# Feed forward's first product: eleven pairs of offsets of the weight parts, a transpose ahead of each unit's products

## The chip, the cores and the metric

The kernel runs on one core of one Trainium2 chip. The metric is the device time of one execution in microseconds (us): 1716.87 us is the median of two runs of the kernel before, 1713.42 and 1720.32 us. All products run on TensorE (PE in the profile). PE first loads 128 x 128 stationary weights (its own row in the profile, PEld) and then streams the moving operand through them, at most 512 columns a time, into a PSUM tile.

## The reference

Two transformer blocks for 256 tokens of width 2048, in float32. The first has attention with a forget gate, a short convolution, pooling and layer norm. The second has gated linear attention, then the feed forward that this change touches, then a gate and a final norm. Cut to that part:

```python
def swiglu(hn, w_in, w_out):
    gate, up = jnp.split(jnp.einsum('btd,de->bte', hn, w_in), 2, axis=-1)
    return jnp.einsum('btf,fd->btd', jax.nn.silu(gate) * up, w_out)

h = h + swiglu(rmsnorm(h, ffn_norm[i]), ffn_w_in[i], ffn_w_out[i])
```

`w_in` is 2048 x 11264: 44 tiles of 128 features for the gate and 44 for the up half.

## The kernel before, in words

Every large product is split so that the fast format fp32r keeps nearly float32 accuracy. A weight tile arrives by DMA as `raw` (128 x 2048, 1 MB), ScalarE (ACT) rounds it to fp32r into `whi` (line 77), and VectorE (DVE) subtracts to get the rest, `wlo` (line 85). The activations lie in SBUF the same way, as a high and a low half side by side (`x[:, k]`, 512 columns: 256 tokens high, 256 tokens low). In the feature-major form, `fm_mm`, which the change touches, a **unit** is one weight tile of 16 slices of 128 x 128. Each slice makes one **pair** of products: the high weights times all 512 columns (line 185), then the low weights times the 256 high columns (line 187). In the token-major form, `tm_mm` (lines 208 to 210), the activations are the stationary operand and the weights move.

A class `Stream` sets the order of everything. Units are listed in program order; the DMA for a unit is issued three units ahead, its high and low part are made two units ahead, and the work that follows a unit's products (its `post`) comes ahead of the next unit's products. Pools of three buffers each hold `raw`, `whi` and `wlo`. Each buffer of `whi` and `wlo` has 64 columns more than the 2048 that are used (`PAD`). In every feature-major unit `whi` starts 16 columns into its buffer (`SHIFT`, line 24; the slice is in line 76) and `wlo` starts at column 0; token-major units have both at 0. A column is 4 bytes on each partition.

The feed forward's first product is 88 units, for f = 0 to 43 a gate and an up, in two parts (48 units for f < 24, then 40), each followed by units of the second product. The function `ffn_in` lists them (lines 1093 and 1094). `gate` and `up` are their posts: ACT and DVE add the two halves of the PSUM tile, scale, apply the activation and split the result into `g`. For f = 0 the token scale is not known yet when the gate is ready; `spread` (line 269) lays it over all partitions with two small fp32 products between the second and the third unit. Ahead of that, inside the first unit, eight transposes (line 1008) of the last quarter of the activations are mixed into the products. The PSUM tiles of these small products come from a pool of four (`axps`), those of the units from another four (`mmps`).

Of the kernel before, what the change touches and what calls it, by code (L numbers as in the profile page):

```python
# [9 lines left out]
F32R = mybir.dt.float32r  # L10
# [7 lines left out]
P = 128  # L18
S = 256
D = 2048  # L20
KT = D // P
UN = 2048

PAD, SHIFT = 64, 16
ALPHA = 2.0 ** 0.25
BIG = 3.0e38

# [7 lines left out]
ORDER = "HFPTL"  # L35
# [4 lines left out]
class Stream:  # L40
# [30 lines left out]
    def _hi(self, w):  # L71
        if w < len(self.ws):
            n, pre_split = self.ws[w][1], self.ws[w][5]
            if pre_split is not None:
                pre_split()
            hi = self.hi_p.tile([P, UN + PAD], F32R, tag="whi", name="whi")[:, self.ws[w][8]:]
            self.nc.scalar.copy(hi[:, :n], self.raw[w][:, :n])  # L77
            self.parts[w] = [hi]

    def _lo(self, w):  # L80
        if w < len(self.ws):
            n, eng = self.ws[w][1], self.ws[w][6]
            t, hi = self.raw.pop(w), self.parts[w][0]
            lo = self.lo_p.tile([P, UN + PAD], F32R, tag="wlo", name="wlo")
            eng.tensor_tensor(lo[:, :n], t[:, :n], hi[:, :n], op=ALU.subtract)  # L85
            self.parts[w].append(lo)
        self._load(w + self.raw_bufs)
# [48 lines left out]
def program(ctx, tc, a, out):  # L136
    nc = tc.nc
# [14 lines left out]
    st = Stream(nc, raw_p, hi_p, lo_p, 3, 2)  # L152

    def mmps():
        return ps_mm.tile([P, 512], F32, tag="mm", name="mm")

    def axps():
        return ps_ax.tile([P, 512], F32, tag="ax", name="ax")

    ident = const.tile([P, P], F32, name="ident")  # L160
# [16 lines left out]
    def fm_mm(ps, hi, lo, x, k0, n, first, last, m=P, zigzag=False):  # L177


        for kk in range(n):  # L180
            w, k = slice(kk * m, (kk + 1) * m), k0 + kk
            if kk and zigzag:
                MM(ps[:, :S], lhsT=lo[:, w], rhs=x[:, k, 0], start=False, stop=False)
            end = last and kk == n - 1
            MM(ps, lhsT=hi[:, w], rhs=x[:, k], start=first and kk == 0, stop=end and zigzag)  # L185
            if not kk or not zigzag:
                MM(ps[:, :S], lhsT=lo[:, w], rhs=x[:, k, 0], start=False, stop=end and not zigzag)  # L187
            for fn in mid.pop(kk, ()):
                fn()

    def join(dst, ps):

        A.copy(dst, ps[:, S:])
        V.tensor_tensor(dst, ps[:, :S], dst, op=ALU.add)  # L194

    def split(x, k, src):

        A.copy(x[:, k, 0], src)
        V.tensor_tensor(x[:, k, 1], src, x[:, k, 0], op=ALU.subtract)
# [9 lines left out]
                MM(ps2[t], lhsT=x[:, k0 + kk, 0, tok], rhs=lo[:, w], start=False, stop=False)  # L209
                MM(ps2[t], lhsT=x[:, k0 + kk, 1, tok], rhs=hi[:, w], start=False, stop=e)  # L210

    def fm_units(srcs, groups, xs, post, lo=None, order=ORDER, zigzag=False):

        box = {}
        for j, (src, (k0, n)) in enumerate(zip(srcs, groups)):
            def mm(hi, lo, j=j, k0=k0, n=n):
                if j == 0:
                    box["ps"] = mmps()
                fm_mm(box["ps"], hi, lo, xs(), k0, n, j == 0, j == len(groups) - 1, zigzag=zigzag)

            st.unit(src, n * P, mm, (lambda: post(box["ps"])) if j == len(groups) - 1 else None, lo=lo, order=order, shift=SHIFT)

    def fm_unit(src, xs, post, lo=None, order=ORDER, zigzag=False):
        fm_units([src], [(0, KT)], xs, post, lo, order, zigzag)

    def tm_units(srcs, groups, xs, post, lo=()):

# [22 lines left out]
    def token_scale(ss, tag="rs"):  # L250

        n = ss.shape[1]
        s = rsp.tile([P, n], F32, tag=tag, name="rs", padded_shape=[P, 2])
        V.tensor_reduce(s, ss, axis=AX.X, op=ALU.add)
        V.tensor_scalar(s, s, 1.0 / D, 1e-6, op0=ALU.mult, op1=ALU.add)
        G.tensor_tensor(s, s, mhalf[:, :n], op=ALU.pow)
        return s

    def spread_prep(s):
        rep = rsp.tile([P, 2, P], F32, tag="rep", name="rep")  # L260
        for t in range(2):
            V.tensor_scalar(rep[:, t, :], ones, s[:, t:t + 1], None, op0=ALU.mult)
        return rep

    def spread(dst, rep):

        ps = axps()
        for t in range(2):
            MM(ps[:, t * P:(t + 1) * P], lhsT=rep[:, t, :], rhs=ident, start=True, stop=True)
        A.copy(dst, ps[:, :S])  # L270
# [43 lines left out]
    xs = lambda: xa  # L314
# [64 lines left out]
    for n, per in ((0, 2), (1, 4)):  # L379
        box = {}  # L380
# [23 lines left out]
    for h in range(8):  # L404
# [53 lines left out]
        def g_post(ps, hb=hb):  # L458
            hb["sg"] = silu2(tb["p"], ps)

        fm_unit(a["w1"][u0], xs, q_post)
        fm_unit(a["w1"][u0 + 1], xs, k_post)
        fm_unit(a["w1"][u0 + 2], xs, g_post)
        u0 += 3

# [128 lines left out]
    hns = lambda: hn["x"]  # L594
# [398 lines left out]
    def residual(ps2, n):  # L993

        for t in range(2):
            h = hx["h"][:, t, n * 512:(n + 1) * 512]
            V.tensor_tensor(h, h, ps2[t], op=ALU.add)
# [28 lines left out]
    def feed_on(n, col):  # L1026

        rows, parts, squares = feed(n, col)
        if n < 3 or col != C_FFN:
            def rest():  # L1030
                rows(0)
                rows(1)
                parts()
                squares()
            st.later(1, rest)
        else:
            mid[1] = [lambda: rows(0)]
            mid[4] = [lambda: rows(1), parts, squares]

    def gla_close():  # L1040
        gB.close()
        alloc_hn()

    os_ = lambda: gx["o"]
    for n in range(4):
        def post(ps2, n=n):
            if n == 0:
                gla_close()
            residual(ps2, n)
            feed_on(n, C_FFN)  # L1050
# [13 lines left out]
    def ffn_in(f, base):  # L1064
        b = {}

        def gate(ps):
            if f == 0:
                b["ps"] = ps
                b["rep"] = spread_prep(token_scale(hx["ss"]))  # L1070
            else:
                gate_body(ps)

        def gate_body(ps):
            ft = hx["ft"]
            b["g"] = ft.tile([P, S], F32, tag="fg", name="fg")
            b["th"] = ft.tile([P, S], F32, tag="fth", name="fth")
            join(b["g"], ps)
            V.tensor_tensor(b["g"], b["g"], sB, op=ALU.mult)
            A.activation(b["th"], b["g"], AF.Tanh, scale=0.5)  # L1080
            V.scalar_tensor_tensor(b["g"], b["th"], 1.0, b["g"], op0=ALU.add, op1=ALU.mult)

        def up(ps):
            if f == 0:
                spread(sB, b["rep"])
                gate_body(b["ps"])
            u = hx["ft"].tile([P, S], F32, tag="fu", name="fu")
            join(u, ps)
            V.tensor_tensor(u, u, sB, op=ALU.mult)
            V.scalar_tensor_tensor(u, b["g"], 0.5, u, op0=ALU.mult, op1=ALU.mult)  # L1090
            split(fx["g"], f - base, u)

        fm_unit(a["ffn_in"][2 * f], hns, gate)
        fm_unit(a["ffn_in"][2 * f + 1], hns, up)

    gs = lambda: fx["g"]
    for part, (f0, f1) in enumerate(((0, F_SPLIT), (F_SPLIT, F_ALL))):
# [5 lines left out]
        w = a["ffn_out%d" % part]  # L1103
# [21 lines left out]
    def ple_post(ps2, n):  # L1125
        c = slice(n * 512, (n + 1) * 512)
        if n == 0:
            V.tensor_scalar(px["hs"], token_scale(hx["ss"]), 0.5, None, op0=ALU.mult)
        th = [px["t"].tile([P, 512], F32, tag="pth%d" % t, name="pth") for t in range(2)]

        def gate(t):
            A.activation(th[t], ps2[t], AF.Tanh, scale=px["hs"][:, t:t + 1])

        def add(t):
            h = hx["h"][:, t, c]
            V.scalar_tensor_tensor(th[t], th[t], 1.0, px["pp"][:, t, c], op0=ALU.add, op1=ALU.mult)
            V.scalar_tensor_tensor(h, th[t], 0.5, h, op0=ALU.mult, op1=ALU.add)

        def square(t):
            h = hx["h"][:, t, c]  # L1140
            A.activation(th[t], h, AF.Square, accum_out=hx["ss"][:, t, n:n + 1])
            if n < 3:
                G.tensor_tensor(h, h, px["fin"][:, c], op=ALU.mult)

        gate(0)
        add(0)
        square(0)
        gate(1)
        if n < 3:
            add(1)  # L1150
            square(1)
            return
        s0 = token_scale(hx["ss"][:, 0:1, :])
        add(1)
        out_rows(0, s0, (0, 1))
        square(1)
        out_rows(0, s0, (3,))
        s1 = token_scale(hx["ss"][:, 1:2, :], "rs1")
        out_rows(0, s0, (2,))
        out_rows(1, s1, (0, 3, 1, 2))  # L1160
# [14 lines left out]
    for n in range(4):  # L1175
        tm_units([a["ple_gate"][n * 4 + j] for j in range(4)], [(j * 4, 4) for j in range(4)], hns,
                 lambda ps2, n=n: ple_post(ps2, n))
# [109 lines left out]
```

## Time and profile before

| | |
|---|---|
| median of two runs | 1716.87 us (1713.42 and 1720.32) |
| the profiled execution | 1713.25 us |
| its span, first to last instruction | 1711.5 us |
| PE busy | 1678.2 us, 98% |
| DVE, ACT busy | 1067.9 us (62%), 797.2 us (47%) |
| granted clock of TensorE, mean | 0.992 |

The profile lists, for each engine, when each instruction started and how long its record is. Records of products overlap, because the next product enters the array while the last one drains; what a product costs in a stream is the distance from its start to the next start. A row like `795.09 0.40 PE L185 MATMUL mm<-hn,whi 128*128 128x512 f32 x1` reads: it started 795.09 us into the span, its record is 0.40 us long, it comes from line 185, wrote a tile `mm` and read `hn` and `whi`, with 128 x 128 weights and 512 columns; x4 at the end would be four like it, merged.

### The profile page before, as it was taken

To read this page: it belongs to the slowest core of one execution; us is meant where nothing else is said; L and a number is where in the kernel's file an instruction comes from. 1 tells how busy PE (TensorE), PEld (TensorE's weight loads), DVE (VectorE), ACT (ScalarE), POOL (GpSimd) and SP (SyncE) were. 2 spreads that over 40 slices of the span, in tenths; PEclk is the share of its full clock that TensorE was granted. 3 is DMA by queue.
4 is the path that set the end of the run, shared out by engine and by line. 5 is a ranking of instruction groups with operands and counts; after the bars stand their busy time and mean duration, and the time that the engine had idled before them with its cause. 6 is when DMAs were issued, how large, how long until landed. Compare 5 with 4: busy or idle time off the path is not lost.

```text
span 1711.5 us, 21258 instructions
## 1 busy us (share of the span) xinstructions
PE 1678.2 (98%) x8890; PEld 1440.7 (84%) x8890; DVE 1067.9 (62%) x1250; ACT 797.2 (47%) x909; POOL 45.1 (3%) x57
## 2 busy tenths in 40 slices
PE   8999999999999999999999999999999999999997
PEld 5888888888777888888888888888888888888886
DVE  4565666655877678657556666664446666655554
ACT  5554544433655455444444444443334444444443
POOL 0400000000000000000000000000000000000011
PEclk9999999999999999999999999999999999999999
DMA  8544455476553334346555555556555555555653
GB/s 276 206 176 182 160 192 179 173 260 251 210 199 135 128 137 148 129 167 237 182 197 172 197 196 189 190 191 206 191 192 193 188 190 193 194 197 197 247 175 119
DMA packets 49313, 322.60 MB, mean 188 GB/s; under 512 B 5625, under 2 KB 5953, under 8 KB 12481
## 3 DMA queue, kind: packets, MB, share of 16 engines
q1 hardware_dynamic: 49216, 321.25, 53.5%
q8 instruction: 69, 1.13, 0.3%
q14 instruction: 28, 0.22, 0.0%
HBM read 314.86 MB, written 6.30 MB: 188 GB/s over the span
## 4 chain that ended last, share of the span: by engine, by line
PE 62%; DVE 6%; ACT 2%; issue 1%; ACTq 0%; POOLq 0%; POOL 0%; DVEq 0%
PE mm L185 22%; PE mm L187 11%; PE mm L208 9%; PE mm L210 9%; PE mm L209 9%; DVE wlo L85 2%; DVE kq L884 1%; PE ax L863 1%; PE mm L917 1%; DVE tl L832 0%; PE ax L1008 0%; ACT km L887 0%; DVE at L872 0%; ACT whi L77 0%; DVE te L828 0%
## 5 line engine op out<-in xcount | busy, mean ns | idle before, releaser
L77 ACT CAST whi<-raw 128x2048 fp32r<-128x2048 f32 (+1 forms) x290 | 546.2, 1884 | 602.3 <-PE mm L210 306.8
L85 DVE TENSOR_TENSOR wlo<-raw,whi 128x2048 fp32r<-128x2048 f32 (+1 forms) x290 | 657.5, 2268 | 211.9 <-ACT whi L77 211.7
L185 PE MATMUL mm<-hn,whi 128*128 128x512 f32 x1920 | 664.5, 393 | 1.5 <-DVE hn L1016 0.8
L187 PE MATMUL mm<-hn,wlo 128*128 128x256 f32 x1920 | 533.5, 278 | 0.0
L185 PEld LDWEIGHTS mm<-hn,whi 128*128 128x128 f32 x1920 | 362.3, 189 | 78.4 <-DVE hn L1016 1.4
L187 PEld LDWEIGHTS mm<-hn,wlo 128*128 128x128 f32 x1920 | 362.9, 189 | 0.2
L185 PE MATMUL mm<-xa,whi 128*128 128x512 f32 x768 | 273.4, 399 | 0.0
L187 PE MATMUL mm<-xa,wlo 128*128 128x256 f32 x768 | 215.8, 281 | 0.0
L185 PEld LDWEIGHTS mm<-xa,whi 128*128 128x128 f32 x768 | 144.2, 188 | 32.8
L187 PEld LDWEIGHTS mm<-xa,wlo 128*128 128x128 f32 x768 | 145.3, 189 | 0.3
L208 PE MATMUL mm<-whi,g 128*128 128x512 f32 x352 | 137.2, 390 | 0.0
L210 PE MATMUL mm<-whi,g 128*128 128x512 f32 x352 | 137.0, 389 | 0.0
L209 PE MATMUL mm<-wlo,g 128*128 128x512 f32 x352 | 137.0, 389 | 0.0
L208 PE MATMUL mm<-whi,hn 128*128 128x512 f32 x256 | 102.5, 400 | 1.8 <-DVE og L194 1.8
L210 PE MATMUL mm<-whi,hn 128*128 128x512 f32 x256 | 101.0, 395 | 0.0
L209 PE MATMUL mm<-wlo,hn 128*128 128x512 f32 x256 | 100.9, 394 | 0.0
L210 PEld LDWEIGHTS mm<-whi,g 128*128 128x128 f32 x352 | 66.1, 188 | 13.7
L208 PEld LDWEIGHTS mm<-whi,g 128*128 128x128 f32 x352 | 66.1, 188 | 13.6
L209 PEld LDWEIGHTS mm<-wlo,g 128*128 128x128 f32 x352 | 66.1, 188 | 13.6
L208 PEld LDWEIGHTS mm<-whi,hn 128*128 128x128 f32 x256 | 49.0, 191 | 12.1 <-DVE og L194 2.3
L210 PEld LDWEIGHTS mm<-whi,hn 128*128 128x128 f32 x256 | 48.9, 191 | 10.4
L209 PEld LDWEIGHTS mm<-wlo,hn 128*128 128x128 f32 x256 | 49.0, 191 | 9.9
(250 smaller groups left out, 1573.1 us busy)
## 6 DMA issues: line engine op xcount, KB each, us to landing
raw<-in_w SPq DMA_DIRECT2D x100, 1024.0 KB, 4.8
raw<-in_ffn_in SPq DMA_DIRECT2D x88, 1024.0 KB, 4.9
raw<-in_ffn_out SPq DMA_DIRECT2D x44, 1024.0 KB, 4.9
raw<-in_w_out SPq DMA_DIRECT2D x16, 1024.0 KB, 5.0
raw<-in_gla_out SPq DMA_DIRECT2D x16, 1024.0 KB, 4.9
raw<-in_ple_gate SPq DMA_DIRECT2D x16, 1024.0 KB, 4.9
raw<-in_w SPq DMA_DIRECT2D x8, 512.0 KB, 5.3
xT<-in_xT SPq DMA_DIRECT2D x8, 256.0 KB, 5.6
```

The lines of the kernel that those rows point to most:

```text
L77: self.nc.scalar.copy(hi[:, :n], self.raw[w][:, :n])
L85: eng.tensor_tensor(lo[:, :n], t[:, :n], hi[:, :n], op=ALU.subtract)
L185: MM(ps, lhsT=hi[:, w], rhs=x[:, k], start=first and kk == 0, stop=end and zigzag)
L187: MM(ps[:, :S], lhsT=lo[:, w], rhs=x[:, k, 0], start=False, stop=end and not zigzag)
L208: MM(ps2[t], lhsT=x[:, k0 + kk, 0, tok], rhs=hi[:, w], start=b, stop=False)
L209: MM(ps2[t], lhsT=x[:, k0 + kk, 0, tok], rhs=lo[:, w], start=False, stop=False)
L210: MM(ps2[t], lhsT=x[:, k0 + kk, 1, tok], rhs=hi[:, w], start=False, stop=e)
L863: MM(ps[:, tok], lhsT=km[:, d, tok], rhs=rhs, start=(d == 0), stop=(d == 1))
L884: V.tensor_tensor(o, o, f, op=ALU.mult)
L917: MM(ps[:, i * S:(i + 1) * S], lhsT=hb["v"][:, j, v], rhs=hb["at"][:, j, :], start=(j == 0), stop=(j == 1))
```

## The change

It does two things to the 88 units of the feed forward's first product.

The offset `SHIFT` becomes a pair, for the high and for the low part, and these units take theirs from a list of eleven: four values of f, that is eight units, share one pair. f = 0 to 3 keep (16, 0). Then come (0, 16), (32, 0), (0, 32), (48, 0), (16, 16), (8, 0), (16, 48), (24, 0), (4, 0) and (16, 32), in columns. All other feature-major units keep (16, 0), all token-major units (0, 0).

And ahead of each of these units' products stands one transpose of the identity matrix (128 x 128, fp32) into a fresh PSUM tile that nobody reads (`apart`).

```diff
-PAD, SHIFT = 64, 16
+PAD, SHIFT = 64, (16, 0)
+SHIFTS = ((16, 0), (0, 16), (32, 0), (0, 32), (48, 0), (16, 16), (8, 0), (16, 48), (24, 0), (4, 0), (16, 32))
...
-            hi = self.hi_p.tile([P, UN + PAD], F32R, tag="whi", name="whi")[:, self.ws[w][8]:]
+            hi = self.hi_p.tile([P, UN + PAD], F32R, tag="whi", name="whi")[:, (self.ws[w][8] or (0, 0))[0]:]
...
-            lo = self.lo_p.tile([P, UN + PAD], F32R, tag="wlo", name="wlo")
+            lo = self.lo_p.tile([P, UN + PAD], F32R, tag="wlo", name="wlo")[:, (self.ws[w][8] or (0, 0))[1]:]
...
-    def fm_units(srcs, groups, xs, post, lo=None, order=ORDER, zigzag=False):
+    def fm_units(srcs, groups, xs, post, lo=None, order=ORDER, zigzag=False, shift=SHIFT, apart=False):
...
                 if j == 0:
                     box["ps"] = mmps()
+                if apart:
+                    nc.tensor.transpose(axps()[:, :P], ident, ident)
                 fm_mm(box["ps"], hi, lo, xs(), k0, n, j == 0, j == len(groups) - 1, zigzag=zigzag)
...
-            st.unit(src, n * P, mm, (lambda: post(box["ps"])) if j == len(groups) - 1 else None, lo=lo, order=order, shift=SHIFT)
+            st.unit(src, n * P, mm, (lambda: post(box["ps"])) if j == len(groups) - 1 else None, lo=lo, order=order, shift=shift)
...
-        fm_unit(a["ffn_in"][2 * f], hns, gate)
-        fm_unit(a["ffn_in"][2 * f + 1], hns, up)
+        fm_unit(a["ffn_in"][2 * f], hns, gate, shift=SHIFTS[f // 4], apart=True)
+        fm_unit(a["ffn_in"][2 * f + 1], hns, up, shift=SHIFTS[f // 4], apart=True)
```

Only PE's order changes: 88 rows are added, and the other engines issue the same instructions in the same order. The first place is the border of the third and the fourth unit of the feed forward on PE, which stands for the borders of all the later units; before, with the names' buffer numbers (`mm` is a unit's PSUM tile, `hn` the activations, and what a row waits for stands behind it):

```order
L187 MATMUL mm_7004<-hn_6429,wlo_6875 128x256
L185 MATMUL mm_7050<-hn_6429,whi_6934 128x512 [waits Activation_49]
L187 MATMUL mm_7050<-hn_6429,wlo_6943 128x256 [waits DVE_49]
L185 MATMUL mm_7050<-hn_6429,whi_6934 128x512
L187 MATMUL mm_7050<-hn_6429,wlo_6943 128x256
```

and now, where lines 185 and 187 have become 187 and 189:

```order
L189 MATMUL mm_7008<-hn_6429,wlo_6875 128x256
L222 MATMUL ax_7057<-ident_85 128x128 [waits PE_49]
L187 MATMUL mm_7056<-hn_6429,whi_6936 128x512 [waits Activation_49]
L189 MATMUL mm_7056<-hn_6429,wlo_6945 128x256 [waits DVE_49]
L187 MATMUL mm_7056<-hn_6429,whi_6936 128x512
```

The transpose has come between the last low product of one unit and the first high product of the next; it waits for PE's own semaphore, and the products wait for ACT and DVE as they did. The second place is the border of the second and third unit, where the spread's two products stood already; now on PE:

```order
L189 MATMUL mm_6949<-hn_6429,wlo_6838 128x256
L273 MATMUL ax_6986<-ident_85,rep_6942 128x128 [waits DVE_49,PE_49]
L273 MATMUL ax_6986<-ident_85,rep_6942 128x128 [waits DVE_49]
L222 MATMUL ax_7009<-ident_85 128x128 [waits PE_49]
L187 MATMUL mm_7008<-hn_6429,whi_6873 128x512
```

Here the transpose comes behind the two products of the spread; before, line 185 followed them at once.

## Rows read from the trace of the kernel before

**Rows 1.** The page: busy time, share and count by engine; granted clock in forty slices.
```profile
PE 1678.2 (98%) x8890; PEld 1440.7 (84%) x8890; DVE 1067.9 (62%) x1250; ACT 797.2 (47%) x909; POOL 45.1 (3%) x57
...
PEclk9999999999999999999999999999999999999999
```
**Rows 2.** Stretches: length, then busy us (count) of PE, PEld, DVE, ACT, POOL; clock, DMA share, GB/s.
```profile
60.00:225.00 165.00, 165.00 (x957) 145.53 (x956) 96.90 (x138) 81.87 (x119) 11.02 (x16) 1.00 0.48 179
...
903.00:1152.00 249.00, 249.00 (x1467) 220.21 (x1466) 169.47 (x210) 118.83 (x141) 0.00 (x0) 1.00 0.56 192
1283.00:1500.00 217.00, 217.00 (x1278) 192.49 (x1277) 145.13 (x177) 102.94 (x118) 0.00 (x0) 1.00 0.57 193
```
**Rows 3.** Timeline of PE in the feed forward: start us, length us, engine, line, instruction.
```profile
949.79 0.39 PE L185 MATMUL mm<-hn,whi 128*128 128x512 f32 x1
...
950.81 0.39 PE L185 MATMUL mm<-hn,whi 128*128 128x512 f32 x1
```
**Rows 4.** Stretches for line 185 alone: length, busy us (count) of PE and PEld, clock.
```profile
225.00:310.00 85.00, 84.92 (x240) 44.98 (x240) 1.00 0.51 186
903.00:1152.00 249.00, 249.00 (x733) 137.43 (x733) 1.00 0.56 192
```
**Rows 5.** Timeline of PE near the end of the linear attention, three pairs on.
```profile
795.09 0.40 PE L185 MATMUL mm<-hn,whi 128*128 128x512 f32 x1
...
796.14 0.39 PE L185 MATMUL mm<-hn,whi 128*128 128x512 f32 x1
```
**Rows 6.** Timeline of PE at one group of three transposes in the first block.
```profile
107.74 0.28 PE L187 MATMUL mm<-xa,wlo 128*128 128x256 f32 x1
107.86 0.49 PE L437 MATMUL ax<-ident,lt 128*128 128x128 f32 x3
...
108.54 0.40 PE L185 MATMUL mm<-xa,whi 128*128 128x512 f32 x1
...
109.24 0.40 PE L185 MATMUL mm<-xa,whi 128*128 128x512 f32 x1
```
**Rows 7.** Timeline of PE at four transposes inside the feed forward's first unit.
```profile
890.55 0.60 PE L1008 MATMUL ax<-ident,h 128*128 128x128 f32 x4
...
891.34 0.39 PE L185 MATMUL mm<-hn,whi 128*128 128x512 f32 x1
...
891.68 0.39 PE L185 MATMUL mm<-hn,whi 128*128 128x512 f32 x1
```
**Rows 8.** Timeline of PE at the spread between the feed forward's second and third unit.
```profile
901.74 0.60 PE L269 MATMUL ax<-ident,rep 128*128 128x128 f32 x4
...
902.53 0.39 PE L185 MATMUL mm<-hn,whi 128*128 128x512 f32 x1
...
902.87 0.39 PE L185 MATMUL mm<-hn,whi 128*128 128x512 f32 x1
```
**Rows 9.** Timeline of PE at a spread in the linear attention.
```profile
775.74 0.61 PE L269 MATMUL ax<-ident,rep 128*128 128x128 f32 x4
...
776.54 0.40 PE L185 MATMUL mm<-hn,whi 128*128 128x512 f32 x1
...
776.89 0.39 PE L185 MATMUL mm<-hn,whi 128*128 128x512 f32 x1
```
**Rows 10.** Line 437: count, length in ns (least, median, most), first and last start us.
```profile
L437 PE MATMUL ax<-ident,lt x24: 270/271/274, 89.4 to 218.7; 128*128 128x128 f32 x24
```
**Rows 11.** Groups by form, 903 to 1152 us: count, busy us, mean ns, idle before.
```profile
L187 PE MATMUL mm<-hn,wlo 128*128 128x256 f32 x734 | 202.6, 276 | 0.0
L187 PEld LDWEIGHTS mm<-hn,wlo 128*128 128x128 f32 x733 | 137.6, 188 | 0.0
...
L85 DVE TENSOR_TENSOR wlo<-raw,whi 128x2048 fp32r<-128x2048 f32 x46 | 105.1, 2284 | 0.0
```
**Rows 12.** Timeline of PE in the second product of the feed forward, token-major.
```profile
1200.06 0.39 PE L208 MATMUL mm<-whi,g 128*128 128x512 f32 x1
1200.29 0.39 PE L209 MATMUL mm<-wlo,g 128*128 128x512 f32 x1
```

More of the change, by code (lines that the diff above doesn't have):

```diff
@@ L218, in mm, with fm_unit @@
                     box["ps"] = mmps()
+                if apart:
+                    nc.tensor.transpose(axps()[:, :P], ident, ident)
                 fm_mm(box["ps"], hi, lo, xs(), k0, n, j == 0, j == len(groups) - 1, zigzag=zigzag)
-            st.unit(src, n * P, mm, (lambda: post(box["ps"])) if j == len(groups) - 1 else None, lo=lo, order=order, shift=SHIFT)
-    def fm_unit(src, xs, post, lo=None, order=ORDER, zigzag=False):
-        fm_units([src], [(0, KT)], xs, post, lo, order, zigzag)
+            st.unit(src, n * P, mm, (lambda: post(box["ps"])) if j == len(groups) - 1 else None, lo=lo, order=order, shift=shift)
+    def fm_unit(src, xs, post, lo=None, order=ORDER, zigzag=False, shift=SHIFT, apart=False):
+        fm_units([src], [(0, KT)], xs, post, lo, order, zigzag, shift, apart)
     def tm_units(srcs, groups, xs, post, lo=()):
```

## The prediction, made before the changed kernel ran

> **What bounds the kernel now.** I read the page first. PE is busy for 98% of the span and everything else for 62% or less [rows 1], and PE works with the granted clock at its full digit in all forty slices. So the end is set by how fast matmuls follow each other, and the next question is which stretch the change touches: the 88 units of the feed forward's first product, in two parts. The table of stretches gives them as 903 to 1152 us (first part) and 1283 to 1500 us (second part): PE is busy in every microsecond of both at granted clock 1.00, DVE for 169.47 of 249.00 us, ACT for 118.83 [rows 2]. Nothing waits there for weights, for a DMA or for PSUM. A unit costs what its 16 pairs of products cost, a 512-column product with the high weight part and a 256-column product with the low one.
>
> A record's length does not tell that cost: the 512-column product is drawn 0.39 us long, and the next product starts 0.23 us after it. What counts is the distance from start to start. In the feed forward three pairs of products take from 949.79 to 950.81, 0.34 us a pair [rows 3]. The stretch bears it out: 733 high products in 249.00 us are 339.7 ns each [rows 4]. The same two instructions with the same weight offsets, (16, 0), run slower elsewhere: between 795.09 and 796.14 us three pairs take 1.05 us, 350 ns each, at the same clock [rows 5], and 225 to 310 us holds 240 pairs in 85.00 us, 354 ns each [rows 4]. So one piece of code has at least two steady patterns, **340 and 350 to 354 ns a pair**, and the stretch that is changed runs wholly in the quick one.
>
> What decides between them? Read the places where another product stands between two units. At 107.86 three transposes; afterwards two pairs take from 108.54 to 109.24 us, 350 ns each [rows 6]. At 890.55 four transposes, and what follows is 891.34 to 891.68, 340 [rows 7]. After the two spreads (fp32 products that lay the token scale over all partitions) it goes both ways: 902.53 to 902.87 is 340 [rows 8], and 776.54 to 776.89 is 350 [rows 9]. Once a pattern is entered it lasts: the first part starts in the quick pattern at 902.53 and is still in it at its end. With nothing between its units, it has no occasion to leave.
>
> **The change, part by part.**
> *The 88 transposes.* The order of PE's instructions gains 88 rows and loses none; the other engines issue what they issued. Their price is in [rows 6]: from the low product at 107.74 to the second high product of the next unit at 108.54 is 0.80 us with three transposes in it. Without them it would be 0.12 (low product to what follows) and 0.35 (a pair), 0.47 us. The remaining 0.33 us are three transposes: 0.11 us each. 88 x 0.11 = **+9.7 us**, all on the path, since PE has no gap that could take them. Another way to it: three in a row are drawn 0.49 us long, the last of them 0.271 [rows 6, 10], so their starts lie 0.22 / 2 = 0.11 apart. It is the lower bound too, as no row shows 128 columns of fp32 in less; the upper one is the whole record, 271 ns, 23.8 us for 88, which the 0.80 us above rules out.
> The Trainium skill, "TensorE: Matmul & The Clock Gate", Part 4, puts a transpose at about 275 ns in one kernel's context and says that the clock does not rise for it; by that sum the term would be 24.2 us. The trace agrees on the length of the record and differs on what it costs in a stream, 0.11 us; and with 24 transposes in it the stretch from 60 to 225 us holds clock 1.00 [rows 2].
> *The waits of the transposes.* Each waits for PE's own semaphore, for the transpose that last wrote its PSUM tile. The pool has four such tiles, so that one is some four units (20 us) old; no engine reads it. PE works in order, so the wait is over before it is met. Nothing; if it did hold PE until the product just before had drained, its cover gone, that would be a record's length less its 0.11 us of start to start, 0.276 - 0.113 = 0.16 us, and 88 x 0.16 = 14 us [rows 11].
> *The broken lock.* Here is the larger part. Each transpose is an occasion to change the pattern, 88 of them where there was one per part. After transposes the trace has nine such places: eight in the first block, the groups of three that make up the 24 records of line 437 [rows 10], of which [rows 6] is one and all eight go on at 350, and the one of [rows 7], which goes on at 340. With the two spreads it is 9 slow of 11. I take 9/11 of the units to run at 350 instead of 340: 0.82 x 88 x 16 x 10 ns = **+11.5 us**. Bounds: nothing, if all fall into the quick pattern; 88 x 16 x 14 ns = 19.7 us at the slowest average that the trace shows, 354.
> *The offsets.* The eight units of f = 0 to 3 keep (16, 0); the other 80 get ten new pairs. No row shows any of these in this product. That the start address matters at all is a guess from two patterns at one address; nearest rows say a pair lies between 340 and 354, whatever set it off, and I use that for all pairs, with a margin for the odd starts (4, 8 and 24 columns).
> *ACT and DVE* write and read the parts at the new starts. A subtraction takes 2284 ns and 46 of them stand in 249 us [rows 11], where DVE is idle for 79.5 us. That cover is 1.7 us a unit: the subtraction could grow to 4.0 us before PE waited for it. ACT idles for half. Nothing, for any of the offsets. No DMA and no tile size changes; the padding of 64 columns holds the largest start, 48.
>
> **Sum.** 1713.25 us (the profiled execution, span 1711.5 and 1.75 around it) + 9.7 + 11.5 = **1734.5 us**. Against the median of the runs shown, 1716.87, this is 1.0% slower. The two runs lie 6.9 us apart; one part in the 350 pattern would make 40 x 16 x 10 ns = 6.4 us (second part) or 7.7 us (first), so the slower may be one that locked badly. The changed kernel settles anew in each unit and should not inherit that.
>
> **Rivals.**
> *Every unit falls into the quick pattern.* The transposes then cost 9.7 us and nothing else: 1723 us. For it speaks that the pattern was entered at 891.34 and 902.53; against it 9 of 11 places. The Trainium skill, "SBUF — State Buffer", section "Who interferes with whom", says that PE reads moving operand and weights through independent ports and never waits on anyone; taken at its word no address could matter and this rival would hold. The 340 and 350 ns of one code at one clock speak against it, though not for a particular cause.
> *Weight loads come to bound at some offsets.* A weight load is drawn 188 ns long [rows 11], and is now hidden. If odd starts stretch it until two loads in a row set the pair, that is 2 x 188 = 376 ns, 36 more than now. For the three odd pairs alone, 24 x 16 x 36 = 13.8 us, the rest at 350 in nine of eleven, 64 x 16 x 8.2 = 8.4: 1713.25 + 9.7 + 13.8 + 8.4 = 1745. For all ten new pairs 80 x 16 x 36 = 46 us: 1769. It passes the 2% line (1751.2) from an average of (1751.2 - 1722.95) / 1408 = 20 ns a pair above 340. No row shows 360.
> *Some offsets are quicker than 340.* That is the side of a gain. A pair at 340 ns is 0.443 ns a column of its 768; a transpose's 128 fp32 columns in 0.1095 us are 0.855, twice 0.428. If the difference, 768 x 0.015 = 12 ns a pair, came from a collision that a new offset removes, 80 units would save 80 x 16 x 12 ns = 15.4 us: 1713.25 + 9.7 - 15.4 = 1707.6, faster by 0.5%. It pays from an average of 9.7 us / 1408 = 6.9 ns a pair under 340. Against it: products with the weights as moving operand, at start 0, also go at 0.23 us per 512 columns [rows 12], so 0.443 looks like the rate of this data type.
>
> **How the numbers follow.** Forecast (transposes in full, most units slow): 0.62, own range 1728 to 1742. All quick: 0.17. Worse than the slowest average seen, through weight loads, through some pairs, or through a wait of PE for itself that does hold it: 0.16, of which 0.07 beyond 1751. Some pairs quicker than 340: 0.05. The range from 1722 to 1748 holds the first two cases and the nearer half of the third. A measurement of this kernel can tell about 2% from no change; by that line: faster 0.01, same 0.92, slower 0.07.
>
> **What would show it.** In the profile after, 88 transposes at 0.11 us each and 88 more PE rows; high products from 907 us on that stand 350 apart in most units, in groups of eight units if the offsets decide and mixed within a group if chance does; DVE, ACT and clock as now. The lock step is wrong if nearly all units stand at 340, and the offset step if one group stands beyond 357. The prediction is wrong if PE shows gaps ahead of a unit's first product, which would be a wait that I costed at nothing.

## The result

| | before | after |
|---|---|---|
| median | 1716.87 us of two runs (1713.42, 1720.32) | 1735.53 us of two runs (1734.56, 1736.50) |
| the profiled execution, its span | 1713.25, 1711.5 us | 1736.50, 1734.7 us |

The ratio is 1.0126, 95% interval 1.0094 to 1.0159; the two medians by themselves divide to 1.0109, inside that interval. So the kernel is slower by 1.1 to 1.3%, with 1734.5 us forecast. The executions of the kernel before lie in two groups, 1711 to 1714 and 1718 to 1722 us, in every set of more than one run; the last experiment shows what parts two such groups in a kernel close to it, and the profiled execution here is of the lower group. Against that execution the two runs after cost 21 and 23 us more.

On the page of the kernel after, PE is busier by 23.2 us and PEld by 17.1 us, of which the weight loads of the 88 transposes are 12.5 (0.142 us each). DVE, ACT and POOL have moved by 0.3 us or less, and the clock row is the same (compare [rows 1]; the share of the span, then the number of instructions):

```profile
PE 1701.4 (98%) x8978; PEld 1457.8 (84%) x8978; DVE 1067.8 (62%) x1250; ACT 796.9 (46%) x909; POOL 45.4 (3%) x57
...
PEclk9999999999999999999999999999999999999999
```

The timeline of PE at the border of two units at (0, 16) (lines 185 and 187 are now 187 and 189, the transpose is line 222), which answers to [rows 3, 6]:

```profile
941.59 0.39 PE L187 MATMUL mm<-hn,whi 128*128 128x512 f32 x1
941.82 0.28 PE L189 MATMUL mm<-hn,wlo 128*128 128x256 f32 x1
941.94 0.27 PE L222 MATMUL ax<-ident 128*128 128x128 f32 x1
941.96 0.48 PE L187 MATMUL mm<-hn,whi 128*128 128x512 f32 x1
...
942.39 0.39 PE L187 MATMUL mm<-hn,whi 128*128 128x512 f32 x1
942.62 0.28 PE L189 MATMUL mm<-hn,wlo 128*128 128x256 f32 x1
942.74 0.39 PE L187 MATMUL mm<-hn,whi 128*128 128x512 f32 x1
```

From the last low product to the second high one, 941.82 to 942.39, are 0.57 us; without the transpose 0.12 + 0.347 = 0.467. So it costs 0.10 to 0.11 us. The transpose starts 0.12 us after the low product, as a high product would, so its wait held nothing. The pair behind it takes 0.35 us at this resolution; over the unit the mean is 346.6 ns.

Stretches for line 187, one for each group of eight units, in the order of the list (length, busy us (count) of PE and of PEld, clock). A group has 128 high products; the count takes in one or two that reach in from a neighbour:

```profile
888.24:936.29 48.05, 46.14 (x129) 24.04 (x129) 1.00 0.51 175
936.29:981.65 45.36, 45.36 (x130) 24.04 (x129) 1.00 0.54 186
981.65:1027.57 45.92, 45.92 (x129) 24.07 (x129) 1.00 0.54 184
1027.57:1073.05 45.48, 45.48 (x130) 24.02 (x129) 1.00 0.54 185
1073.05:1118.58 45.53, 45.53 (x130) 24.07 (x129) 1.00 0.54 185
1118.58:1164.46 45.88, 45.88 (x129) 24.05 (x128) 1.00 0.53 184
1295.24:1341.05 45.81, 45.81 (x129) 24.05 (x129) 1.00 0.53 183
1341.05:1386.94 45.89, 45.89 (x129) 24.13 (x129) 1.00 0.54 184
1386.94:1432.29 45.35, 45.35 (x130) 24.07 (x129) 1.00 0.55 186
1432.29:1477.95 45.66, 45.66 (x129) 24.02 (x129) 1.00 0.54 185
1477.95:1523.69 45.74, 45.74 (x129) 24.08 (x128) 1.00 0.54 184
```

Eight units in the quick pattern would be 8 x 16 x 0.340 = 43.52 us. From the second on, every group lies 1.8 to 2.4 us above that, of which 8 x 0.11 = 0.9 are the transposes. The first stretch holds in addition the eight transposes of line 1008 and the spread, as before.

Where the 23.2 us are: 88 transposes, 9.7 us. The rest from the pairs. The mean distance of the pairs in the middle of a unit (pairs 5 to 15, from the starts in the trace, which are kept to 1 ns) is 350.0 ns over the eleven groups, 340.0 before: 86 x 16 x 10.0 ns = 13.8 us (86, since the first two units ran at 350 before). The sum is 23.5.

What each pair of offsets shows, with the transposes (the kernel after) and without (the second experiment below), ns a pair. Each is a mean over eleven distances; where long and short distances take turns, it can be off by 1 ns:

| high, low | after: eight units | without transposes |
|---|---|---|
| (16, 0) | 350 six times, 340 once (first unit left out) | 340 behind the spread |
| (0, 16) | 346.6 | 346.6 |
| (32, 0) | 352 | 352 |
| (0, 32) | 346.6 four times, 350 four times | 346.7 |
| (48, 0) | 350 seven times, 340 once | 340 |
| (16, 16) | 353.4 | 353.4 |
| (8, 0) | 351 | 351 |
| (16, 48) | 352.6 to 353.4 | 353.3 |
| (24, 0) | 346.6 seven times, 350 once | 346.7 |
| (4, 0) | 350 | 350.2 |
| (16, 32) | 350 four times, 353.4 four times | 349.5 |

### The profile page after: what moved, and what is told of

Same layout as the page of the kernel before. It is cut to its first block, busy times and chain, and to the rows that moved or that the text cites. A ratio compares the mean times of both kernels' runs of the same rounds, so it can differ in the third digit from the quotient of the medians.

```text
span 1734.7 us, 21433 instructions
## 1 busy us (share of the span) xinstructions
PE 1701.4 (98%) x8978; PEld 1457.8 (84%) x8978; DVE 1067.8 (62%) x1250; ACT 796.9 (46%) x909; POOL 45.4 (3%) x57
## 4 chain that ended last, share of the span: by engine, by line
PE 62%; DVE 6%; ACT 2%; issue 1%; ACTq 0%; POOLq 0%; POOL 0%; DVEq 0%
PE mm L187 22%; PE mm L189 11%; PE mm L210 9%; PE mm L212 9%; PE mm L211 9%; DVE wlo L87 2%; DVE kq L888 1%; PE ax L867 1%; PE mm L921 1%; PE ax L222 1%; DVE tl L836 0%; PE ax L1012 0%; ACT km L891 0%; DVE at L876 0%; ACT whi L79 0%
## 5 line engine op out<-in xcount | busy, mean ns | idle before, releaser
L79 ACT CAST whi<-raw 128x2048 fp32r<-128x2048 f32 (+1 forms) x290 | 546.0, 1884 | 625.9 <-PE mm L212 304.0
L87 DVE TENSOR_TENSOR wlo<-raw,whi 128x2048 fp32r<-128x2048 f32 (+1 forms) x290 | 657.4, 2268 | 212.3 <-ACT whi L79 212.0
L187 PE MATMUL mm<-hn,whi 128*128 128x512 f32 x1920 | 687.6, 400 | 1.3 <-ACT vh L910 0.7
L189 PE MATMUL mm<-hn,wlo 128*128 128x256 f32 x1920 | 539.8, 281 | 0.0
L196 DVE TENSOR_TENSOR fu<-mm,fu 128x256 f32<-128x256 f32 x44 | 18.7, 424 | 71.7 <-ACT fu L195 71.6
```

## Experiments

The diffs are against the changed kernel, save where the text says otherwise.

**The transposes alone.** All eleven pairs become (16, 0).

```diff
-SHIFTS = ((16, 0), (0, 16), (32, 0), ...)
+SHIFTS = ((16, 0),) * 11
```

> The change without its offsets: all 88 units keep (16, 0), the 88 transposes stay. Theory A (a transpose costs 0.11 us and makes the next unit settle its pattern anew, mostly at 350 ns a pair; offsets only choose between slow patterns): 1713.3 + 9.7 + 88 x 16 x 10 ns x 0.82 to 1.0 = 1734.5 to 1737 us, and starts 350 apart in at least seven units of ten in all eleven groups. Theory B (the offsets are what slows the pairs, a transpose only costs its 0.11 us): 1723 us, 340 ns a pair everywhere.

Measured: 1732.64 us (four runs, 1730.96 to 1733.87), before 1712.9; ratio 1.0109 (1.0080 to 1.0137). The transposes alone cost 19.7 us, where theory B had 9.7. Theory A's time, 1734.5 to 1737 us, was missed by 2 us: the share of slow units was 0.75 and not 0.82 or more, and one of the eleven groups had only five slow units of eight. In the profiled execution the quick ones come in a fixed turn: from the twelfth unit on, every fourth unit runs at 340 ns and the three between at 350; 22 of the 88 are quick. Groups repeat to 0.01 us (line 187, two groups of eight units; what follows the length is as above):

```profile
1027.61:1073.00 45.39, 45.39 (x129) 24.04 (x129) 1.00 0.55 186
1073.00:1118.39 45.39, 45.39 (x130) 24.04 (x129) 1.00 0.54 186
```

43.52 + 8 x 0.11 + 6 x 16 x 0.010 = 45.36: six of eight slow.

**The offsets alone.** The two lines with the transpose are taken out; the list of pairs stays.

```diff
-                if apart:
-                    nc.tensor.transpose(axps()[:, :P], ident, ident)
```

> The change without its transposes: ten new pairs of offsets, nothing between the units. Theory A (a pattern lasts until another product comes between): the quick pattern that is entered ahead of the third unit is carried through all groups, 340 ns a pair, 1713 to 1717 us. Theory B (each pair of offsets has its own pattern and takes it up by itself): the ten groups run at the 346 to 353 ns that they show in the changed kernel, 80 x 16 x 9.9 ns = 12.7 us more, 1726 us.

Measured: 1723.87 us (seven runs, 1722.94 to 1725.71), before 1712.9; ratio 1.0063 (1.0045 to 1.0081). Theory A falls as far as it says that a pattern is carried on whatever the offsets. Stretches for line 187 of (0, 16) to (16, 16), in the order of the list:

```profile
935.72:980.10 44.38, 44.38 (x130) 24.04 (x129) 1.00 0.57 191
980.10:1025.16 45.06, 45.06 (x130) 24.07 (x129) 1.00 0.55 187
1025.16:1069.54 44.38, 44.38 (x129) 24.03 (x129) 1.00 0.56 190
1069.54:1113.09 43.55, 43.55 (x130) 24.03 (x129) 1.00 0.57 193
1113.09:1158.18 45.09, 45.09 (x129) 23.95 (x128) 1.00 0.55 187
```

The first row is (0, 16): 44.38 us / 128 = 346.7 ns a pair; (32, 0) is 352.0, (0, 32) 346.7, (48, 0) 340.2 and (16, 16), from the starts, 353.4. The pattern changes with the first unit of a group and holds in all eight, and in the program nothing but the addresses of the weights has changed there. So this run shows that the addresses matter; that a pair has only one pattern it does not show, and a later run shows the contrary. Nine of the ten new pairs have not one quick unit, here or with the transposes. Theory B gave 12.7 us for ten slow groups; one, (48, 0), is quick, and 11.0 us were measured.

**Two transposes in all**, ahead of the gates of f = 8 and f = 32, (16, 0) throughout.

```diff
-        fm_unit(a["ffn_in"][2 * f], hns, gate, shift=SHIFTS[f // 4], apart=True)
-        fm_unit(a["ffn_in"][2 * f + 1], hns, up, shift=SHIFTS[f // 4], apart=True)
+        fm_unit(a["ffn_in"][2 * f], hns, gate, shift=SHIFTS[f // 4], apart=f in (8, 32))
+        fm_unit(a["ffn_in"][2 * f + 1], hns, up, shift=SHIFTS[f // 4])
```

> The kernel before with two transposes in all, ahead of the gates of f = 8 and f = 32, at (16, 0) throughout. Theory A: pairs at 340 ns up to each transpose and at 350 ns from it to the end of its part, 32 units in the first and 24 in the second: 56 x 16 x 10 ns + 0.2 = 9.2 us, 1722.5 us; if one of the two places happens to stay quick, 4 to 5 us less. Theory C (a transpose disturbs only the unit that follows it): 2 x 0.27 us, 1714 us.

Measured: 1722.69 us (nine runs, 1720.43 to 1723.11), before 1712.9; ratio 1.0049 (1.0034 to 1.0064). The timeline of PE at the first of the two:

```profile
975.93 0.39 PE L187 MATMUL mm<-hn,whi 128*128 128x512 f32 x1
...
976.27 0.39 PE L187 MATMUL mm<-hn,whi 128*128 128x512 f32 x1
976.50 0.28 PE L189 MATMUL mm<-hn,wlo 128*128 128x256 f32 x1
976.62 0.27 PE L222 MATMUL ax<-ident 128*128 128x128 f32 x1
...
977.08 0.39 PE L187 MATMUL mm<-hn,whi 128*128 128x512 f32 x1
...
977.78 0.39 PE L187 MATMUL mm<-hn,whi 128*128 128x512 f32 x1
```

340 ns before it, two pairs in 0.70 us after it, and the starts stay so for all 32 units to the end of the part; the 24 units behind the second one likewise. Two products of 0.11 us cost 9 us in the pairs (56 x 16 x 10 ns; the medians differ by 9.8), so theory C falls. This is the prediction's lock by itself, and with nothing between the units and one address it does last.

**An extra product of the units' own kind** in place of the transpose, (16, 0) throughout.

```diff
-                    nc.tensor.transpose(axps()[:, :P], ident, ident)
+                    MM(axps()[:, :S], lhsT=lo[:, :P], rhs=xs()[:, 0, 0], start=True, stop=True)
```

> The transposes replaced by one extra product of the units' own kind (fp32r, the unit's first low slice times 256 columns, into a PSUM tile that nobody reads), (16, 0) throughout. The time has 88 x 0.113 = 10.0 us of added products in any case. Theory A1 (what breaks the pattern is the fp32 product, which takes another rate): 340 ns a pair stay, 1723 us. Theory A2 (any interruption of high, low, high, low breaks it): most units at 350 ns, 1735 to 1737 us.

Measured: 1732.8 us (four runs, 1731.71 to 1733.89), before 1712.9; ratio 1.0110 (1.0082 to 1.0138). So it takes neither an fp32 product nor the transpose mode. The timeline of PE:

```profile
1025.92 0.39 PE L187 MATMUL mm<-hn,whi 128*128 128x512 f32 x1
1026.14 0.28 PE L189 MATMUL mm<-hn,wlo 128*128 128x256 f32 x1
1026.26 0.28 PE L222 MATMUL ax<-hn,wlo 128*128 128x256 f32 x1
1026.38 0.40 PE L187 MATMUL mm<-hn,whi 128*128 128x512 f32 x1
...
1027.08 0.40 PE L187 MATMUL mm<-hn,whi 128*128 128x512 f32 x1
```

A unit at 340 ends, the extra low product takes 0.12 us, and the next unit goes at 350. Here every third unit is quick, in a fixed turn, so theory A1 falls. A2's time, 1735 to 1737 us, was missed by 2 us, as only two units in three are slow.

**Two transposes ahead of each unit**, (16, 0) throughout.

```diff
                 if apart:
                     nc.tensor.transpose(axps()[:, :P], ident, ident)
+                    nc.tensor.transpose(axps()[:, :P], ident, ident)
```

> As e1 (all at (16, 0)), with two transposes ahead of each unit instead of one. The direct price of a transpose in a stream is 0.11 us: 88 x 0.11 = 9.7 us more than e1, 1742 us, if the share of quick units stays near a quarter; between 1739 (half quick) and 1746 us (none quick). If a transpose cost its whole record of 0.27 us, 24 us more than e1, 1756 us.

Measured: 1745.27 us (two runs), 12.6 us more than with one, which ran in another set; ratio to before 1.0152 (1.0117 to 1.0186). Now no unit is quick (349.8 ns in 86 of 88, from the starts), so 21 units or so lose 160 ns each, 3.4 us, and 88 more transposes have 9.2 us left: 0.105 us each. Its timeline says the same:

```profile
1076.36 0.28 PE L189 MATMUL mm<-hn,wlo 128*128 128x256 f32 x1
1076.47 0.27 PE L222 MATMUL ax<-ident 128*128 128x128 f32 x1
1076.58 0.27 PE L223 MATMUL ax<-ident 128*128 128x128 f32 x1
...
1077.04 0.40 PE L187 MATMUL mm<-hn,whi 128*128 128x512 f32 x1
```

0.11 us lie between the starts of the two, and 0.68 us from low to second high product less 0.12 and 0.35 leave 0.21 for both.

**Eleven other pairs**, with the transposes.

```diff
-SHIFTS = ((16, 0), (0, 16), (32, 0), ...)
+SHIFTS = ((0, 0), (40, 0), (0, 48), (48, 16), (32, 16), (12, 0), (56, 0), (48, 32), (0, 24), (20, 0), (0, 8))
```

> The changed kernel, transposes and all, with eleven other pairs: (0, 0), (40, 0), (0, 48), (48, 16), (32, 16), (12, 0), (56, 0), (48, 32), (0, 24), (20, 0), (0, 8). Theory D (only the distance of the two starts counts): (32, 16) and (48, 32) behave as (16, 0), three units of four at 350 and one at 340, (48, 16) as (32, 0) at 352, (0, 0) as (16, 16) at 353. Theory E (both starts count, each pair has a pattern of its own): no such agreement, every group within 340 to 354. The time is 1722 to 1742 us either way; a group at 340 throughout would be of use.

Measured: 1734.63 us (two runs); ratio to before 1.0090 (1.0055 to 1.0124). Theory D falls: (32, 16) stands at 346.6 to 347.3 ns, (48, 32) and (48, 16) at 346.7, (0, 0) at 346.4 from its fourth unit on, none like the pair of the same distance. The others: (40, 0) 349.4, (0, 48) 346.6 to 351.2, (12, 0) 349.5, (56, 0) 344.2 to 353.4, (0, 24) 346.6 or 351.7, (20, 0) 348.9, (0, 8) 346.0 to 347.7. None reaches 340 and none passes 353.6. Theory E's other half, one pattern to each pair, does not hold either: (0, 48), (56, 0) and (0, 24) each show two or more.

**The high products first, then the low ones**, in all 168 feature-major units, against the kernel before.

```diff
-            MM(ps, lhsT=hi[:, w], rhs=x[:, k], start=first and kk == 0, stop=end and zigzag)
+            MM(ps, lhsT=hi[:, w], rhs=x[:, k], start=first and kk == 0, stop=False)
...
+        for kk in range(n):
+            w, k = slice(kk * m, (kk + 1) * m), k0 + kk
+            MM(ps[:, :S], lhsT=lo[:, w], rhs=x[:, k, 0], start=False, stop=last and kk == n - 1)
```

> The kernel before, with the sixteen high products of a unit first and its sixteen low ones behind them, in all 168 feature-major units, (16, 0). Theory F (it is the change between long and short products that can settle in a slow pattern; a run of equal products keeps 0.227 us for 512 columns as the token-major units do): 340 ns a pair also in the 80 units outside the feed forward, 80 x 16 x 10 ns = 12.8 us less, 1700 us. Theory G (every weight load can collide, whatever stands beside it, and a low product of 0.113 us is too short for the load of the next): the low runs go at 0.12 us or more, 350 ns a pair or worse in all units, 1713 + 88 x 16 x 10 ns = 1727 us or more.

Measured: 1731.34 us (four runs, 1730.11 to 1732.42); ratio to before 1.0071 (1.0047 to 1.0094), in a set where most runs of before lay in their upper group; against the lower it is 1.1%. The timeline, with equal products merged:

```profile
1000.26 3.90 PE L182 MATMUL mm<-hn,whi 128*128 128x512 f32 x16
1004.00 2.06 PE L187 MATMUL mm<-hn,wlo 128*128 128x256 f32 x16
1005.89 0.40 PE L182 MATMUL mm<-hn,whi 128*128 128x512 f32 x1
```

3.74 us / 16 = 234 ns a high product and 1.89 / 16 = 118 a low one, 352 together: both kinds are slow, each in a run of its own kind. Theory F falls, G's number holds; its reason, that a weight load is too long for the product beside it, is not shown. The slow pattern does not need the change between long and short products.

**(0, 16) outside the feed forward**, (16, 0) in it, no transposes.

```diff
-PAD, SHIFT = 64, (16, 0)
+PAD, SHIFT = 64, (0, 16)
...
-SHIFTS = ((16, 0), (0, 16), (32, 0), ...)
+SHIFTS = ((16, 0),) * 11
...
-                if apart:
-                    nc.tensor.transpose(axps()[:, :P], ident, ident)
```

> No transposes; the feed forward's first product keeps (16, 0), the 80 other feature-major units get (0, 16), which showed 346.6 ns a pair with and without transposes. If that pattern is the pair's own, these units go from 350 to 346.6 ns: 80 x 16 x 3.4 ns = 4.4 us less, 1708.5 us. If the pattern belongs to the feed forward's surroundings (its activations, its neighbours), they stay at 350 and the time at 1713 us.

Measured: 1716.14 us (twelve runs) beside 1720.4 (seventeen) in the same set; ratio 0.9981 (0.9965 to 0.9998). Both kernels fall into two groups there: this one 1709.2 to 1710.7 and 1715.4 to 1718.1, before 1711.7 to 1714.4 and 1719.5 to 1721.4. In the trace all 79 units outside that run undisturbed stand at 346.7, where in the kernel before 72 stood at 350 to 354, six at 340 and one, disturbed there, at 357. The forecast was 4.4 us less. The medians give 4.3; the lower groups by themselves are 2.9 us apart, the upper ones 4.0. In the trace, which caught an execution of the lower group, the first part ran at 340 (a stretch for line 187):

```profile
903.00:1149.00 246.00, 246.00 (x724) 135.75 (x725) 1.00 0.56 192
```

246.00 us / 724 are 339.8 ns, and the units from the third on stand at 340.0 by their starts.

**Taking turns.** No transposes; the feed forward's groups alternate between (0, 16) or (0, 32) and (16, 0) or (48, 0). Against the kernel with (0, 16) outside, above:

```diff
-SHIFTS = ((16, 0),) * 11
+SHIFTS = ((0, 16), (16, 0), (0, 16), (48, 0), (0, 32), (16, 0), (0, 16), (48, 0), (0, 16), (16, 0), (0, 16))
```

> No transposes. The feed forward's groups of eight units take turns: (0, 16), (16, 0), (0, 16), (48, 0), (0, 32), (16, 0) in the first part, (0, 16), (48, 0), (0, 16), (16, 0), (0, 16) in the second; all other feature-major units have (0, 16). Theory H (with nothing between the units, the pattern that a pair settles in is set by the pattern before it, so the same step gives the same result each time): both steps from (0, 16) to (16, 0) end alike, both to (48, 0) end alike, and a step that ends at 340 ns ends there in all eight units. Theory I (which pattern is taken is chance at each entry): the two steps of a kind can differ. Groups at (0, 16) show 346.6 in any case. Time: 1710 + (40 x 16 x 6.6 = 4.2) = 1714 us if all four groups at (16, 0) or (48, 0) are quick, 1720 us if none is.

Measured in one run each: 1717.02 us, before 1712.98. Stretches for line 187: from (0, 16) into (16, 0), into (48, 0), into (48, 0) again, and into (16, 0) again:

```profile
930.82:975.62 44.80, 44.80 (x129) 24.04 (x129) 1.00 0.54 188
...
1020.00:1063.52 43.52, 43.52 (x129) 24.02 (x129) 1.00 0.57 194
...
1328.53:1372.06 43.53, 43.53 (x129) 24.02 (x129) 1.00 0.57 193
1416.44:1459.96 43.52, 43.52 (x129) 24.02 (x129) 1.00 0.56 194
```

128 pairs in 44.80 us are 350.0 ns, in 43.52 us 340.0. The step to (48, 0) was quick both times, the step to (16, 0) once. So theory H does not hold as it was put: the pair before does not settle it for (16, 0). For (48, 0) it was left to the next run. The steps out of (48, 0) and out of (0, 32) in the first part:

```profile
1063.52:1108.33 44.81, 44.81 (x129) 23.99 (x129) 1.00 0.54 188
1108.33:1152.00 43.67, 43.67 (x125) 23.13 (x124) 1.00 0.54 182
```

The first row is (0, 32) behind (48, 0): 44.81 us / 128 are 350.1 ns, in all eight units, where the same pair stood at 346.7 behind (32, 0) in the run without transposes. The second is (16, 0) behind (0, 32), at 353.0 from the starts. So a pair of offsets has several patterns, three at (16, 0), and what came before has a part in which one it takes up.

**A lead, then (48, 0).** (0, 16) outside the feed forward and in its first units (f = 0, 1 and 24), (48, 0) in all later ones. The diff leaves out what the kernel with (0, 16) outside has too:

```diff
+LEAD = (0, 1, F_SPLIT)
...
-        fm_unit(a["ffn_in"][2 * f], hns, gate, shift=SHIFTS[f // 4], apart=True)
-        fm_unit(a["ffn_in"][2 * f + 1], hns, up, shift=SHIFTS[f // 4], apart=True)
+        fm_unit(a["ffn_in"][2 * f], hns, gate, shift=SHIFT if f in LEAD else (48, 0))
+        fm_unit(a["ffn_in"][2 * f + 1], hns, up, shift=SHIFT if f in LEAD else (48, 0))
```

> No transposes. (0, 16) in the 80 other feature-major units and in the lead of each part of the feed forward (four units, two units), then (48, 0) for the other 82 units. Theory H (the step from (0, 16) to (48, 0) ends in the quick pattern every time): 340 ns a pair in all units behind the leads, 346.7 in the others: 1713 - 4.4 + 6 x 16 x 6.7 ns = 1709.5 us, and the executions of this kernel lie within 3 us, while those of the kernel before lie in two groups some 8 us apart (1711 to 1714, 1719 to 1721). Theory I (chance at each entry): executions of this kernel too lie in groups, 6 to 8 us apart for a part at 350.

And beside it, on the same chip, the kernel with (0, 16) outside and (16, 0) inside once more, the same as above in every line:

> The kernel with (0, 16) outside the feed forward and (16, 0) inside, once more beside e10, to see on one chip whether its executions lie in two groups. Theory H: yes, since the entry into the feed forward's first product is left as it was: near 1709.5 us where both parts run at 340 ns, near 1716 us where one part runs at 350 (40 to 46 units x 16 x 10 ns = 6.4 to 7.4 us). Theory I: as e10, two groups in both.

Measured: 1708.66 us for the lead (nine runs, 1707.83 to 1710.00), 1712.55 for the other (twelve runs: six at 1707.8 to 1710.1, six at 1715.0 to 1717.9), 1712.49 for the kernel before (twenty: seventeen at 1711.1 to 1714.1, three at 1718.2 to 1720.4). The lead's ratio to before is 0.9970 (0.9955 to 0.9984), 0.3% quicker, and its nine runs lie in one group, which is as quick as the lower group of the other. The other's ratio is 1.0000 (0.9985 to 1.0014): half of its runs lie in its upper group and only three of twenty before; the lower groups are 3.4 us apart, near the 2.9 of the earlier set. Theory H had said so of both, one group for the lead and two for the other. The lead kernel's two parts behind the lead-in units (line 187):

```profile
908.00:1147.00 239.00, 239.00 (x704) 131.92 (x704) 1.00 0.58 196
1290.00:1495.00 205.00, 205.00 (x604) 113.17 (x604) 1.00 0.57 193
```

239.00 us / 703 and 205.00 / 603 are 340.0 ns (leaving out a record that reaches in). This time the profile of the other kernel caught an execution of its upper group, 1715.04 us. Stretches for line 187, its two parts:

```profile
898.00:1154.00 256.00, 256.00 (x733) 137.37 (x732) 1.00 0.55 187
1285.00:1502.00 217.00, 217.00 (x639) 119.84 (x639) 1.00 0.57 193
```

256.00 us / 732 = 349.7 ns (leaving out a record that reaches in) and 217.00 / 638 = 340.1: the first part ran slow from its second unit, where the stretch begins, to its last. 46 units that are quick otherwise make 46 x 16 x 10 ns = 7.4 us, the distance of the two groups' means (1708.8 and 1716.2). So one kernel has been profiled in both groups: its entry through the spread was quick in the execution of 1710.30 us and slow in that of 1715.04, and one entry decided for 46 units. For the kernel before, whose upper group no profile caught, the same is likely and not shown.

## Why the prediction was right, step by step

*The bound.* Right: PE stayed busy without a gap through both parts, and its 23.2 us more are the 23.2 us by which the span is longer.

*Transposes, 9.7 us.* Right: 0.10 to 0.11 us each in the profile after, 0.105 by doubling them. The Trainium skill's 275 ns ("TensorE: Matmul & The Clock Gate", Part 4) is again the length of the record, 0.27 us, and not the price in a stream.

*Waits, DMA, ACT, DVE at nothing.* Right. The rounding and the subtraction kept their mean length, 1884 and 2268 ns over the whole kernel on both pages.

*The broken lock, 11.5 us.* Right in kind, and shown by two transposes that cost 9 us. Its size rested on 9 slow places in 11. One was overlooked: behind the other four transposes of that unit (line 1008), 889.85 to 890.20 us is 350 ns, which makes 10 in 12; over all small products between or inside the feature-major units that trace has 37 slow places in 43 that no wait disturbs. At (16, 0) alone three units in four are slow: 0.75 x 88 x 16 x 10 ns = 10.6 us. The turn of four, and of three with another product, suggests that this is no chance that averages out but a state that each unit hands on. It could also be the four PSUM tiles and the three weight buffers, which come round in the same turns; no run changed those.

That an entered pattern lasts with nothing between the products was put too simply: a wait of PE can end it as well. The quick pattern of [rows 7] was lost in the same unit, in the kernel before, over two waits of 0.39 and 0.41 us for the activations, with no other product between:

```profile
894.27 0.50 PE L185 MATMUL mm<-hn,whi 128*128 128x512 f32 x1 [0.39 <-DVE hn L1016]
...
896.14 0.39 PE L185 MATMUL mm<-hn,whi 128*128 128x512 f32 x1
...
896.49 0.39 PE L185 MATMUL mm<-hn,whi 128*128 128x512 f32 x1
```

896.14 to 896.49 is 350 ns, and so it stayed until the spread.

*The offsets, nothing beyond that.* This step was wrong, though small in the sum. "I use that for all pairs" treated the ten new pairs as (16, 0) over again; "that the start address matters at all" was called a guess. The offsets alone cost 11 us: in nine of the ten new pairs no unit was quick. With the transposes the two causes overlap, since a unit can be slow only once: 10.6 us for the transposes' share and 11 for the offsets' became 13.8 together, 3 more than with (16, 0). That the sum still came within 1 us of the median and 2 us of the profiled execution is in part luck: the share of slow units was taken 0.9 us too high at (16, 0), the offsets 3.2 us too low. Of the prediction's two signs both came: in six groups all units stand alike to 1 ns, in five they mix. Its sign of a wrong offset step, a group beyond 357, did not come.

The Trainium skill, "SBUF — State Buffer", section "Who interferes with whom", has PE wait for no one; here the same products at one clock go from 346.7 to 352.0 ns a pair by moving the low weights by 64 bytes and the high ones by 128. Whether another engine or PE's own reads make that difference, no run shows.

*The side remark on the two runs.* That the slower run before had one part in the 350 pattern fits the 7.4 us between the two groups of that other kernel in the last experiment, and the changed kernel, which settles anew in each unit, did not inherit it: its two runs lie 1.9 us apart.

*The rivals.* All quick: held for one unit in four at (16, 0). Weight loads as the bound: no group passed 353.4 ns, odd starts were no worse than others (350, 351 and 346.6), and the records of weight loads kept their length. Quicker than 340: none of 22 pairs.

## What to carry to other kernels

Measure a stream of products by the distance of their starts, not by the length of records, and look whether the same code has two steady distances; if so, what stands between the units, a small product or a wait, can decide for all that follow, and one small product can cost more than forty times its own price (0.11 us that made 32 units lose 0.16 us each). Where weights are split into two buffers, their start addresses are a parameter worth a survey that gives one group of units to each choice within one kernel; what a group shows is a pattern that its choice took up there, not the only one it has. A choice that took up the same middling pattern wherever it was used here, (0, 16) at 346.7 ns, can beat one that is best but often missed (340 or 350), and an entry that ended the same way in all nine runs also took the spread out of the executions.

## What was not expected of the hardware

The steady patterns are short repeats whose length goes in steps of one size. Some are one distance: 340.0 ns at (16, 0) and (48, 0), 346.7 at (0, 32) and 353.3 at (16, 16), in the run without transposes. Others are several distances in turn. By the starts in that trace, (16, 32) takes 344 and 356 ns, 700 together; (32, 0) takes 352, 358, 352, 347 and 351, 1760 together; (8, 0) six distances of 348 to 358, 2106.7 together; (4, 0) six, 2100. The 350 of (16, 0) is two in turn, 349 and 351 or 348 and 352, again 700.

At the granted clock of 1.00, 2.4 GHz, 6.67 ns are 16 cycles, and all of these sums are whole numbers of them: 51, 52 and 53 for the single distances, then 105, 264, 316 and 315. Repeats of the eleven other pairs fit as well: 262 for the five distances of (40, 0) and of (12, 0), 157 for the three of (20, 0), 155 for the three of (56, 0) in its quickest units, 1033.3 ns. A single start need not lie on such a step, 348 ns does not; the whole repeat does. In the run without transposes the repeats also go on unbroken from unit to unit, through all three weight buffers.

So a pattern seems to last because its repeat meets, at the same point each time, something that comes back every 16 cycles. That is read from the numbers, not shown: which unit keeps such a grid, why a move of the weights by 16 columns makes another repeat, and why the step from (0, 16) to (16, 0) ended in two ways stay open. No run here moved the activations or took the weight loads away.
